# Index scores and attention logits taking two PSUM banks in turn, with four conditioning blocks moved in front of attention

## The chip, the cores and the metric

The kernel runs on one core of a Trainium2 chip. The metric is the device time of one execution in microseconds (us). The core's engines, as the profile names them, are TensorE (PE, matmuls and transposes), VectorE (DVE), ScalarE (ACT), GpSimd (POOL) and SyncE (SP, which only issues DMA transfers here). Each takes its instructions in a fixed order. Matmuls write to PSUM, which the kernel uses as eight banks of 128 x 512 floats.

## The reference, cut to what matters

Two blocks run one after the other on 256 tokens of width 1024. The change lies in the first one and in what feeds the second:

```
dots = relu(einsum('bqhd,bsd->bqhs', qi, ki));  score = einsum('bqhs,bqh->bqs', dots, wi) * idx_scale
sel  = top_k(score, 64)                              # visible keys only
logits = q.k * scale + rel_bias[bucket];  probs = softmax(logits over sel);  y_att = (probs @ v) @ w_att_out
y_conv = silu(layer_norm(depthwise_conv(a * sigmoid(g)) + conv_b)) @ w_conv_out
x = x + (sigmoid(gates0) * y_att + sigmoid(gates1) * y_conv) @ w_out
...                                                  # 128 gathered experts per token, a gated projection
sh1, sc1, g1, sh2, sc2, g2 = split(silu(c) @ ada_w + ada_b)   # "ada"; the same for c_ctx
...                                                  # second block: scan mixer and FFN, modulated by these
```

Here silu(c) @ ada_w is a vector of 1024 times a matrix of 1024 x 6144, for two vectors (c and c_ctx) in the first four of its twelve blocks ("rows" in the code) of 512 columns, and for c alone in the others.

## The kernel before

The program is written in code order, and a scheduler turns this order into a priority: it sets ahead of time the fixed sequence of each engine. Instructions from further down move up where an engine would otherwise wait. A tile whose buffer is still in use makes its writer wait, so buffer counts and PSUM banks shape these sequences.

PSUM is handed out by `bank(tag)`: four banks for large products ("mm"), two for transposes ("tp"), and one each under the tags "ac0" and "ac1". With the tag "ac" it takes "ac0" and "ac1" in turn:

```
in_turn = cycle(("ac0", "ac1"))
if tag == "ac":
    tag = next(in_turn)
```

The first block's code, in order, after the projections for the index:

- `index(t)` for the two halves of 128 tokens (t = 0, 1): four groups of two matmuls (L637) into bank "ac0"; ACT applies relu (L641, tile rl, two buffers), DVE sums heads (L646, L648) and finds the top 64 (L656, L657), giving the mask negm.
- the GLU products, then q, k and v (L211 with tiles wr and big; L600 are the transposes of q and k).
- `attention(t)`: SP loads the bias (L566, one buffer of tile bias, so the second half's load waits until PE has read the first half's); four groups of logits (L675 bias, L676 q.k) into "ac0"; DVE adds the mask into the tile lg (L678, one buffer); DVE takes the maximum (L682), ACT the exponentials (L685); for each head PE transposes (L691), ACT copies (L693) and PE multiplies by v (L695) into `po`, a bank "ac0" too; DVE normalizes (L698, tile ot); L249/L251 transpose it into aT.
- the gates: 64 matmuls of 512 columns (L211), taken by DVE (L753) and ACT (L754).
- the depthwise convolution yc on DVE (L759, L762), 120 multiply-adds.
- four blocks of `ada_row` for both vectors: SP loads wada in pieces of 512 KB (L398, two buffers, four for each block); ACT makes the first product (L405) and DVE 14 multiply-adds (L407) into two acc tiles (one buffer each); PE sums over partitions with eight one-column matmuls (L412, shown by the trace as 16) into bank "ac1".
- the convolution's layer norm (L767 to L784), two more blocks of ada for one vector, then att_out (L211 with aT), conv_out (L211 with yc) and the product with w_out. I call what begins with the aT products behind attention the last stretch.

The trace shows each float32 matmul as two records; "x8" in its rows is four matmuls.

Of the kernel before, what the change touches and what calls it, by code (L numbers as in the profile page):

```python
# [92 lines left out]
def block_kernel(ctx: ExitStack, tc: tile.TileContext, I, out):  # L93
# [21 lines left out]
    def bank(tag="mm", bufs=4, shape=(128, 512), name=None):  # L115
        if tag == "ac":
            tag = next(in_turn)
        if tag in ("ac0", "ac1"):
            bufs = 1
        return ps.tile(list(shape), F32, tag=tag, bufs=bufs, name=name or tag)  # L120
# [20 lines left out]
    def V(n):  # L141
        o, w = _V[n]
        return vec[:, o:o + w]
# [243 lines left out]
    def run(*gens):  # L387
        for _ in together(*gens):
            pass
# [156 lines left out]
    with ExitStack() as st:  # L546
# [82 lines left out]
        def index(t):  # L629

            S = 128 * (t + 1)
            score = p1.tile([128, 256], F32, tag="score", name="score", bufs=1)
            for g in range(2):
                for s in range(2):
                    p = bank("ac0")
                    for b in range(2):
                        nc.tensor.matmul(p[:, b * S:(b + 1) * S],  # L637
                                         qiT[s * 64:(s + 1) * 64, 2 * g + b, t * 128:(t + 1) * 128],
                                         kiT[s * 64:(s + 1) * 64, :S], start=True, stop=True)
                    rl = p1.tile([128, 512], F32, tag="rl", name="rl", bufs=2)  # L640
                    nc.scalar.activation(rl[:, :2 * S], p[:, :2 * S], AF.Relu)  # L641
                    for b in range(2):
                        h = 2 * (2 * g + b) + s
                        r = rl[:, b * S:(b + 1) * S]
                        if h == 0:
                            nc.vector.tensor_scalar(score[:, :S], r, wi[:, t, 0:1], None, op0=OP.mult)  # L646
                        else:
                            nc.vector.scalar_tensor_tensor(score[:, :S], r, wi[:, t, h:h + 1], score[:, :S],  # L648
                                                           op0=OP.mult, op1=OP.add)
            nc.vector.scalar_tensor_tensor(score[:, :S], score[:, :S], idx_scale, vis[:, t, :S],  # L650
                                           op0=OP.mult, op1=OP.add)
            work = p1.tile([128, 256], F32, tag="work", name="work", bufs=1)
            m8 = sm.tile([128, 8], F32, tag="m8", name="m8", bufs=2)
            cur = score
            for _ in range(8):
                nc.vector.max(out=m8, in_=cur[:, :S])  # L656
                nc.vector.match_replace(out=work[:, :S], in_to_replace=m8, in_values=cur[:, :S], imm_value=GONE)  # L657
                cur = work
            negm = p1.tile([128, 256], F32, tag="negm", name="negm", bufs=2)
            nc.vector.tensor_tensor(negm[:, :S], work[:, :S], score[:, :S], op=OP.is_equal)  # L660
            nc.vector.tensor_scalar(negm[:, :S], negm[:, :S], -1.0e30, None, op0=OP.mult)
            NM[t] = negm

        def attention(t):
# [3 lines left out]
            lg = p1.tile([128, H, S], F32, tag="lg", name="lg")  # L668
            for g in range(2):
                for s in range(2):  # L670
                    p = bank("ac0")
                    for b in range(2):
                        h = 2 * (2 * g + b) + s
                        o = p[:, b * S:(b + 1) * S]
                        nc.tensor.matmul(o, flip, bias[t][:, h], start=True, stop=False)  # L675
                        nc.tensor.matmul(o, qT[s * 64:(s + 1) * 64, 2 * g + b, t * 128:(t + 1) * 128],  # L676
                                         kT[s * 64:(s + 1) * 64, 2 * g + b, :S], start=False, stop=True)
                    nc.vector.tensor_tensor(lg[:, 4 * g + s:4 * g + s + 3:2, :],  # L678
                                            p[:, :2 * S].rearrange("p (s k) -> p s k", s=2),
                                            negm[:, None, :S].to_broadcast([128, 2, S]), op=OP.add)  # L680
# [3 lines left out]
            for h in range(H):  # L684
                nc.scalar.activation(lg[:, h], lg[:, h], AF.Exp, bias=nmx[:, h:h + 1], accum_out=se[:, h:h + 1])  # L685
            nc.vector.reciprocal(se, se)
            po = bank("ac0")
            for h in range(H):
                tr = tp_bank()
                for j in range(t + 1):  # L690
# [20 lines left out]
        nc.vector.tensor_scalar(qg8, V1("qg"), 0.125, None, op0=OP.mult)  # L711
        for t in range(NT):
            index(t)

        ohb = p1.tile([32, 512], F32, tag="sq", name="ohb", bufs=2)
        nc.sync.dma_start(out=ohb, in_=I["oh"])
# [8 lines left out]

        u = p1.tile([128, 4, TAPS - 1 + 256], F32, tag="u", name="u")
        nc.vector.memset(u[:, :, :TAPS - 1], 0.0)
        sc2 = scv.rearrange("p k s -> p (k s)")
        nc.scalar.activation(sc2, V("c"), AF.Sigmoid)
        nc.vector.tensor_tensor(sc2, sc2, V("c"), op=OP.mult)  # L730
        for j in range(4):
            p = bank()
            lin1(hT, I["w_glu"][2 * j], 256, p[:, :256])
# [6 lines left out]
        lin2(hT, 8, [W[4 * 2 + s] for s in range(4)], both,  # L740
             lambda t, p: nc.scalar.activation(vt[:, t], p, AF.Copy))

        pada = pool("pada", stack=st)
        for t in range(NT):
            attention(t)

# [11 lines left out]
        for j in range(4):  # L758
            nc.vector.tensor_scalar(yc[:, j], u[:, j, 0:256], cw[:, j, 0:1], V1("cb")[:, j:j + 1],  # L759
                                    op0=OP.mult, op1=OP.add)  # L760
            for k in range(1, TAPS):
                nc.vector.scalar_tensor_tensor(yc[:, j], u[:, j, k:k + 256], cw[:, j, k:k + 1], yc[:, j],  # L762
                                               op0=OP.mult, op1=OP.add)
        run(chain(*[ada_row(pada, j, 2) for j in range(4)]))
        pm = bank()
        for j in range(4):
            nc.tensor.matmul(pm[:, :256], mean, yc[:, j], start=j == 0, stop=j == 3)  # L767
# [15 lines left out]
        warm(AF.Sqrt, sgc[:, 0, 0:1])  # L783
        nc.vector.tensor_tensor(yc, yc, sgc, op=OP.mult)  # L784
        cT = yc,
        run(chain(*[ada_row(pada, j, 1) for j in range(4, 6)]))


        mix = sgt[:, :, :D]
# [1035 lines left out]
```

## Time and profile before

| | us |
|---|---|
| runs of the kernel before (median of 3; lowest to highest) | 1593.75; 1590.28 to 1598.25 |
| the profiled execution, its own time | 1593.02 |
| its span in the trace | 1591.3 |
| PE busy in the span | 1363.7 (86%) |
| DVE, POOL, ACT busy | 1139.2, 600.4, 516.4 |
| mean granted clock of PE | 0.899 of full speed |

The span is what the trace covers; 1.7 us of the execution's own time lie around it. A busy share is a mean over very different stages: the first 278 us hold the first block's attention and convolution, some 1070 us behind 300 are the gathered experts and the scan, and the last 200 us the FFN. The granted clock is the share of full speed that PE was given.

### The profile page before, as it was taken

The numbers are of one execution on the slowest core, as the hardware profiler recorded it, in microseconds if no ns is written. First come the engines' busy times: TensorE is split into PE (matmuls) and PEld (weight loads), VectorE is DVE, ScalarE is ACT, GpSimd is POOL, SyncE is SP. The second block draws the span as 40 slices with busy tenths as digits, with TensorE's granted clock in tenths as the row PEclk, the third lists the DMA queues.
The fourth block names the chain that finished last, engine by engine and source line by source line (L and its number), as shares of the span: only waits on it lengthen the run. The fifth ranks groups of instructions, "written<-read, shape, count | busy, mean of one in ns | idle before, by whom it ended". The sixth has DMA issues, their size and how long they took to land. (4 is left out here: it accounts for less than half of the span.)

```text
span 1591.3 us, 26450 instructions
## 1 busy us (share of the span) xinstructions
PE 1363.7 (86%) x10140; PEld 889.3 (56%) x10140; DVE 1139.2 (72%) x2495; ACT 516.4 (32%) x1290; POOL 600.4 (38%) x599
## 2 busy tenths in 40 slices
PE   7999979888878888887884979988679898599997
PEld 5744554666435554545432335645344577399997
DVE  3991573699969888989665687787842966456676
ACT  3122230332243333333233242233232223244543
POOL 0000001245555655565542564254500211356663
PEclk9999959999988888878897989879889889799999
DMA  9545463698898999896997999979987541446561
GB/s 352 187 146 167 137 213 111 254 351 329 322 388 304 392 370 368 329 351 266 416 416 308 398 402 357 362 276 380 408 315 274 178 142 57 170 132 188 181 189 53
DMA packets 90197, 435.12 MB, mean 273 GB/s; under 512 B 9996, under 2 KB 14620, under 8 KB 57304
## 3 DMA queue, kind: packets, MB, share of 16 engines
q0 software_dynamic: 36864, 268.45, 42.8%
q1 hardware_dynamic: 52488, 163.67, 30.0%
q8 instruction: 80, 1.31, 0.3%
q10 hardware_dynamic: 720, 1.31, 0.2%
q14 instruction: 45, 0.37, 0.1%
HBM read 428.39 MB, written 5.01 MB: 272 GB/s over the span
## 5 line engine op out<-in xcount | busy, mean ns | idle before, releaser
L875 POOL DMA_INDIRECT G<-in_experts,eidx x256 | 335.2, 1309 | 356.9 <-DVE x L909 229.3
L880 DVE SCALAR_TENSOR_TENSOR G<-G,h 128x1024 f32<-128x1024 f32 x256 | 322.7, 1272 | 18.4 <-DMA G<-in_experts,eidx 14.9
L905 PE MATMUL ac<-G,dg 128*128 128x512 f32 x504 | 280.3, 705 | 51.4 <-ACT dg L903 51.1
L905 PEld LDWEIGHTS ac<-G,dg 128*128 128x128 f32 x504 | 108.6, 226 | 189.1 <-issue 115.0
L909 DVE SCALAR_TENSOR_TENSOR x<-G,ga,x 128x1024 f32<-128x1024 f32 (+1 forms) x131 | 169.8, 1297 | 1.9
L889 ACT ACTIVATE gd<-dots,gate 128x1 f32<-128x1 f32 x256 | 74.0, 290 | 276.9 <-DVE G L880 271.8
L200 POOL TENSOR_TENSOR wl<-wr,wh 128x1024 fp32r<-128x1024 f32 x50 | 122.4, 2463 | 109.5 <-ACT wh L198 105.8
L211 PE MATMUL mm<-wr,big 128*128 128x512 f32 (+1 forms) x352 | 146.6, 570 | 0.0
L211 PEld LDWEIGHTS mm<-wr,big 128*128 128x128 f32 x352 | 64.2, 192 | 71.8 <-issue 69.7
L407 DVE SCALAR_TENSOR_TENSOR acc<-wada,scv,acc 128x512 f32<-128x512 f32 x112 | 82.9, 770 | 28.9 <-DMA wada<-in_ada 21.7
L211 PE MATMUL mm<-bigl,wh 128*128 128x256 f32 x352 | 99.5, 283 | 1.1 <-DVE bigl L345 1.1
L211 PE MATMUL mm<-bigh,wh 128*128 128x256 f32 x352 | 99.6, 284 | 0.4 <-DVE bigh L344 0.4
L211 PE MATMUL mm<-bigh,wl 128*128 128x256 f32 x352 | 99.1, 283 | 0.0
L799 POOL TENSOR_TENSOR sgt<-sgt 128x512 f32<-128x512 f32 x4 | 5.0, 1271 | 242.4 <-DVE sgt L798 242.4
L1638 DVE SCALAR_TENSOR_TENSOR facc<-mm,vec,facc 128x189 f32<-128x189 f32 (+2 forms) x176 | 75.4, 430 | 25.1 <-ACT facc L1631 20.8
L198 ACT ACTIVATE wh<-wr 128x1024 fp32r<-128x1024 f32 x66 | 69.6, 1059 | 71.8 <-PE tp L211 25.4
L211 PEld LDWEIGHTS mm<-bigl,wh 128*128 128x128 f32 x352 | 67.3, 191 | 1.9 <-DVE bigl L345 1.4
L211 PEld LDWEIGHTS mm<-bigh,wh 128*128 128x128 f32 x352 | 67.5, 192 | 1.4 <-DVE bigh L344 0.6
L211 PEld LDWEIGHTS mm<-bigh,wl 128*128 128x128 f32 x352 | 67.2, 191 | 0.4
L211 PE MATMUL mm<-wr,Xh 128*128 128x512 f32 x144 | 66.2, 609 | 0.0
L903 ACT ACTIVATE dg<-ident,ga 128x128 f32<-128x128 f32 x126 | 44.0, 393 | 28.6 <-DVE ga L892 23.3
L762 DVE SCALAR_TENSOR_TENSOR yc<-u,vec,yc 128x256 f32<-128x256 f32 x120 | 52.3, 475 | 0.3
(481 smaller groups left out, 2688.5 us busy)
## 6 DMA issues: line engine op xcount, KB each, us to landing
wr<-in_w_in SPq DMA_DIRECT2D x56, 512.0 KB
wada<-in_ada SPq DMA_DIRECT2D x48, 512.0 KB
wr<-in_ffn_up SPq DMA_DIRECT2D x44, 512.0 KB
wr<-in_ffn_down SPq DMA_DIRECT2D x22, 512.0 KB
wr<-in_w_att SPq DMA_DIRECT2D x16, 512.0 KB
wr<-in_w_gates SPq DMA_DIRECT2D x16, 512.0 KB
wr<-in_w_ple_gate SPq DMA_DIRECT2D x16, 512.0 KB
wr<-in_w_peer_q SPq DMA_DIRECT2D x14, 512.0 KB
```

The source lines that it names most:

```text
L198: nc.scalar.activation(wh[:, :n], w[:, :n], AF.Copy)
L200: e.tensor_tensor(wl[:, :n], w[:, :n], wh[:, :n].bitcast(F32), op=OP.subtract)
L211: nc.tensor.matmul(o, a, b, start=start and i == 0, stop=stop and i == len(l) - 1)
L407: nc.vector.scalar_tensor_tensor(acc[i], wv, c, acc[i], op0=OP.mult, op1=OP.add)
L762: nc.vector.scalar_tensor_tensor(yc[:, j], u[:, j, k:k + 256], cw[:, j, k:k + 1], yc[:, j], op0=OP.mult, op1=OP.add)
L875: ins = nc.gpsimd.indirect_dma_start(out=b, out_offset=None, in_=I["experts"], in_offset=bass.IndirectOffsetOnAxis(ap=eidx[t, h][:, n:n + ...
L880: nc.vector.scalar_tensor_tensor(b[:, :D], b[:, :D], 1.0, h2[t], op0=OP.mult, op1=OP.mult, accum_out=dots[:, n - g:n - g + 1])
L889: nc.scalar.activation(dg_[:, n:n + 1], dots[:, n:n + 1], AF.Copy, scale=gate[t, h][:, g + n:g + n + 1])
L903: nc.scalar.activation(dg, ident, AF.Copy, scale=c)
L905: nc.tensor.matmul(pacc[q], dg, v[:, q * 512:(q + 1) * 512], start=first and n == to_pe[0], stop=h == H - 1 and n == TOPK - 4)
L909: end = nc.vector.scalar_tensor_tensor(x[:, t, q], v[:, q], c, x[:, t, q], op0=OP.mult, op1=OP.add).ins
L1638: nc.vector.scalar_tensor_tensor(o, pg_[:, a0 + dy:a1 + dy, b0 + dx:b1 + dx], fw[:, j, k_:k_ + 1], o, op0=OP.mult, op1=OP.add)
```

## The change

Three tags become "ac": the index groups, the logit groups and `po` take both banks in turn. The silu of c, the pool of ada and ada's first four blocks stand right behind `index` in the code, with the tag "ac" too, instead of behind the convolution; the last two blocks keep their place and take "ac". The arithmetic is the same. Behind the change, code lines have numbers higher by 1 to 5 up to L763 and the same numbers from L767 on; rows of the kernel before go by its own lines.

```
 def index(t): ...
-                    p = bank("ac0")
+                    p = bank("ac")
...
 def attention(t): ...
-                    p = bank("ac0")
+                    p = bank("ac")
...
-            po = bank("ac0")
+            po = bank("ac")
...
         for t in range(NT):
             index(t)
+        sc2 = scv.rearrange("p k s -> p (k s)")
+        nc.scalar.activation(sc2, V("c"), AF.Sigmoid)
+        nc.vector.tensor_tensor(sc2, sc2, V("c"), op=OP.mult)
+        pada = pool("pada", stack=st)
+        run(chain(*[ada_row(pada, j, 2, tag="ac") for j in range(4)]))
...
-        sc2 = scv.rearrange("p k s -> p (k s)")
-        nc.scalar.activation(sc2, V("c"), AF.Sigmoid)
-        nc.vector.tensor_tensor(sc2, sc2, V("c"), op=OP.mult)
...
-        pada = pool("pada", stack=st)
...
-        run(chain(*[ada_row(pada, j, 2) for j in range(4)]))
...
-        run(chain(*[ada_row(pada, j, 1) for j in range(4, 6)]))
+        run(chain(*[ada_row(pada, j, 1, tag="ac") for j in range(4, 6)]))
```

The scheduler's sequences change well beyond these lines. On PE, at the end of the gates, the sequence of before has the first softmax's transposes (L691) and products with v (L695, bank ac_668) between gate matmuls (L211 mm<-wr,big), and the first ada block's sums (L412, ac_1101) behind them:

```order
L211 MATMUL mm<-wr,big 128x512 x12
L691 MATMUL tp<-ident,lg 128x128 x2
L211 MATMUL mm<-wr,big 128x512 x10
L695 MATMUL ac_668<-vt,pT 128x64 x2
L691 MATMUL tp<-ident,lg 128x128 x2
L211 MATMUL mm<-wr,big 128x512 x5
L412 MATMUL ac_1101<-cst,acc 128x1 x5
```

In the changed kernel the sums of ada's first four blocks (L412, ac_407 to ac_518) stand further up, among the products for q, k, v and the gates. At the end of the gates PE's sequence now reads as follows; ac_798 is the last logit group of the first half, ac_868 the first one of the second half, ac_816 the first half's product with v:

```order
L211 MATMUL mm<-wr,big 128x512 x5
L767 MATMUL mm<-yc,mean 128x256 x4
L675 MATMUL ac_798<-bias,flip 128x128
L676 MATMUL ac_798<-kT,qT 128x128
L675 MATMUL ac_798<-bias,flip 128x128
L676 MATMUL ac_798<-kT,qT 128x128
L773 MATMUL mm<-sqc,mean 128x256 x4
L691 MATMUL tp<-ident,lg 128x128 x2
L675 MATMUL ac_868<-bias,flip 128x256
L676 MATMUL ac_868<-kT,qT 128x256
L675 MATMUL ac_868<-bias,flip 128x256
L676 MATMUL ac_868<-kT,qT 128x256
```

So the last logits and the whole first softmax moved behind the gates, and the second half's first logits, which need the second bias, stand in front of the first half's products with v (L695, the next row).

On DVE, around the second half's maximum (L682 nmx), the sequence of before mixes the mask additions (L678) with ada's multiply-adds (L407):

```order
L407 SCALAR_TENSOR_TENSOR acc<-wada,scv,acc 128x512 x7
L678 TENSOR_TENSOR lg<-ac_738,negm 128x2x256
L407 SCALAR_TENSOR_TENSOR acc<-wada,scv,acc 128x512 x2
L682 TENSOR_REDUCE nmx<-lg 128x8
L407 SCALAR_TENSOR_TENSOR acc<-wada,scv,acc 128x512 x3
L686 RECIPROCAL se<-se 128x8
L364 TENSOR_TENSOR mcol<-ac_1175,vec 128x4 x2
L407 SCALAR_TENSOR_TENSOR acc<-wada,scv,acc 128x512 x14
L698 TENSOR_TENSOR ot<-ac_756,se 128x512
```

In the changed kernel the same place reads:

```order
L678 TENSOR_TENSOR lg<-ac_868,negm 128x2x256
L779 TENSOR_SCALAR yc<-yc,vec_172 128x256 x4
L698 TENSOR_TENSOR ot<-ac_816,se 128x512
L678 TENSOR_TENSOR lg<-ac_880,negm 128x2x256
L784 TENSOR_TENSOR yc<-yc,sgc 128x1024
L678 TENSOR_TENSOR lg<-ac_874,negm 128x2x256
L794 TENSOR_TENSOR sgt<-mm,sgt 128x512
L678 TENSOR_TENSOR lg<-ac_886,negm 128x2x256
L682 TENSOR_REDUCE nmx<-lg 128x8
```

No multiply-add of ada stands in front of that maximum any more; seven (of the sixth block) stand behind it. SP's sequence has ada's wada loads of the first four blocks among the loads for the gates, and the second bias behind seven wada, four att_out and three conv_out loads that follow the last gate loads. In the stages behind the first block the sequences of all engines differ in many places too, though no code there changed.

## Rows read from the trace of the kernel before

**Rows 1.** The page: its head.
```profile
span 1591.3 us, 26450 instructions
```

**Rows 2.** Windows by stage; columns: stretch, length, busy time of each engine, granted clock, DMA.
```profile
40.00:182.00 142.00, 142.00 (x458) 78.71 (x456) 86.31 (x233) 29.32 (x65) 0.00 (x0) 1.00 0.53 163
182.00:233.00 51.00, 39.05 (x158) 28.48 (x157) 41.03 (x66) 19.63 (x41) 0.00 (x0) 0.68 0.56 185
233.00:278.00 45.00, 44.66 (x126) 21.55 (x126) 16.08 (x26) 3.00 (x5) 4.99 (x4) 0.95 0.38 123
...
300.00:1367.00 1067.00, 876.70 (x7802) 539.24 (x7802) 826.37 (x1776) 345.35 (x977) 475.65 (x534) 0.87 0.85 328
```

**Rows 3.** Windows of 4 us around attention, same columns.
```profile
184.00:188.00 4.00, 3.47 (x17) 2.56 (x17) 4.00 (x8) 2.79 (x4) 0.00 (x0) 1.00 0.35 115
...
196.00:200.00 4.00, 4.00 (x24) 2.93 (x24) 2.73 (x7) 3.77 (x4) 0.00 (x0) 1.00 0.32 126
200.00:204.00 4.00, 2.00 (x5) 0.66 (x4) 3.28 (x6) 2.56 (x4) 0.00 (x0) 0.50 0.18 44
...
236.00:240.00 4.00, 4.00 (x8) 1.59 (x8) 2.96 (x4) 0.00 (x0) 0.00 (x0) 0.80 0.47 120
```

**Rows 4.** Timeline of PE, end of the gates: start, length, instructions, idle before.
```profile
151.46 0.38 PE L675 MATMUL ac<-bias,flip 128*128 128x128 f32 x2
...
172.23 0.55 PE L695 MATMUL ac<-vt,pT 128*128 128x64 f32 x4
...
172.85 4.46 PE L211 MATMUL mm<-wr,big 128*128 128x512 f32 x10
...
184.53 1.99 PE L773 MATMUL mm<-sqc,mean 128*128 128x256 f32 x8 [1.66 <-ACT sqc L770]
```

**Rows 5.** Timeline of PE, attention(1): same columns.
```profile
189.20 3.70 PE L211 MATMUL mm<-wr,aT 128*128 128x512 f32 x8
...
196.07 1.95 PE L412 MATMUL ac<-cst,acc 128*128 128x1 f32 x16
197.88 0.68 PE L675 MATMUL ac<-bias,flip 128*128 128x256 f32 x2
...
202.73 1.22 PE L675 MATMUL ac<-bias,flip 128*128 128x256 f32 x2 [2.00 <-DVE lg L678]
...
212.71 1.18 PE L691 MATMUL tp<-ident,lg 128*128 128x128 f32 x4 [5.31 <-ACT lg L685]
213.68 3.52 PE L412 MATMUL ac<-cst,acc 128*128 128x1 f32 x16
...
227.51 3.81 PE L412 MATMUL ac<-cst,acc 128*128 128x1 f32 x16 [1.42 <-DVE acc L407]
...
232.97 5.96 PE L211 MATMUL mm<-wr,aT 128*128 128x512 f32 x8 [0.69 <-ACT aT L251]
```

**Rows 6.** Timeline of DVE: maximum of attention(0).
```profile
153.59 1.22 DVE L682 TENSOR_REDUCE nmx<-lg 128x8 f32<-128x1024 f32 x1
```

**Rows 7.** Timeline of DVE, attention(1).
```profile
209.74 2.28 DVE L682 TENSOR_REDUCE nmx<-lg 128x8 f32<-128x2048 f32 x1
...
222.73 5.39 DVE L407 SCALAR_TENSOR_TENSOR acc<-wada,scv,acc 128x512 f32<-128x512 f32 x8 [1.10 <-DMA wada<-in_ada]
228.04 0.68 DVE L698 TENSOR_TENSOR ot<-ac,se 128x512 f32<-128x512 f32 x1
```

**Rows 8.** Timeline of ACT: exponentials of attention(0), a table load.
```profile
154.84 0.40 ACT L685 ACTIVATE lg<-lg,nmx 128x128 f32<-128x128 f32 x1 [4.82 <-DVE nmx L682]
...
184.49 1.28 ACT L775 ACT_TABLE_LOAD   x1
```

**Rows 9.** Timeline of SP's queue: DMA issues.
```profile
152.71 0.38 SPq L566 DMA_DIRECT2D bias<-brd  x1
...
181.62 24.06 SPq L398 DMA_DIRECT2D wada<-in_ada  x6
```

**Rows 10.** Window behind the issue of the second bias, columns as in Rows 2.
```profile
152.70:157.50 4.80, 4.80 (x13) 2.29 (x14) 1.65 (x2) 2.65 (x14) 0.00 (x0) 1.00 0.86 243
```
## Prediction

> **What bounds the kernel now.** I read the windows by stage first [rows 2]. From 40 to 182 us PE is busy all the time at full clock, so that stretch is as long as its matmuls. From 182 to 233 PE is busy for only 39.05 of 51.0 us and its granted clock is .68: this stretch, attention's second half, is paced by waits and by a slow clock. From 233 to 278 PE is again nearly always busy (44.66 of 45). Then comes the long stretch of gathered experts and scan, which the change does not touch in code.
>
> The 4 us windows [rows 3] show that the clock is binary here: 1.00 up to 200 us, .50 from 200 (1.2 GHz in place of 2.4 GHz) and 1.00 again only within the window from 236 on. The timeline of PE [rows 4, 5] shows what stands in between. The gates end with the row at 172.85 (4.46 us long), so at 177.2. PE waits 1.66 us for the conv's square, 2.00 us for DVE to empty the single logits bank, 5.31 us for the second softmax, 1.42 us for ada's DVE work and 0.69 us for aT. Between these waits stand three rows of one-column ada matmuls: 1.95 us at full clock, 3.52 and 3.81 at half. The last stretch starts at 232.97. I measure the change by how far this start moves.
>
> **The change, part by part.** All times below start from the profiled execution (1593.02 us, of which the span is 1591.3 [rows 1]). The median of the runs is 0.7 us higher, and I add that at the end.
>
> *Gates.* The sums of ada's first four blocks now stand in front of the end of the gates. One costs 197.88 - 196.07 = 1.8 us at full clock [rows 5], four cost 7.2. They delay the gates' end; in exchange the first half's last logit group (1.6 us, four rows from 151.46 on [rows 4]) and the transposes and products with v among the last gate matmuls (172.23 to 172.85, .6) leave. The gates end at 177.2 + 7.2 - 2.2 = 182.2. This holds if the acc tiles are ready in time. DVE was busy for 86.31 of 142 us in this stretch [rows 2]; the 42 multiply-adds of blocks 2 to 4 cost 42 x .67 = 28 us (5.39 us for eight [rows 7]), which makes 114 of 142. There is room on average. With such durations along the two sequences I estimate that the second block's acc is ready between 110 and 115 us and PE at its sums at 117: 2 us of margin at the tightest place. I take no wait, and at most 5 us.
>
> *From the gates to the second half's logits.* PE does the mean (1.8 us; the row of the same shape at 184.53 has 1.99 with its tail [rows 4]) to 184.0, and the last logits to 185.6. DVE adds the mask, to 186.2, and takes the maximum (1.22 us [rows 6]), to 187.4. The conv's subtraction and square take some 2.4 us (an estimate from the wait in front of 184.53), to 186.4; PE's second mean runs to 188.4. ACT loads its table (1.28 us) and makes eight exponentials in some .39 us each [rows 8], 187.7 to 190.9, then another table and a root, to some 192.6, and only then copies for the product with v.
>
> The second half's first logit group needs the second bias. SP issues that load when PE has read the first bias, at 185.6; in the kernel before the same load (8 x 256 floats on 128 partitions, 1.05 MB) was issued at 152.71 [rows 9], and the 4.8 us behind that moved 4.8 x 243 KB = 1.17 MB in all, with the DMA engines .86 busy [rows 10]. I take 4.6 us, bounded by 3.7 (the same at a share of 1) and 8.6 (half of that rate). So the group runs from 190.2 to 192.7. The products with v stand behind it in PE's sequence, but their copies come at 192.6 anyway: this wait hides behind ACT. They go at ACT's pace, I estimate .4 us for each head, to 196.0.
>
> *Second half's logits.* The next group (in the bank that the first logits leave) starts at 196.4, when DVE has written lg, which has one buffer and is free after the last transpose. A group is 2.5 us at full clock. The third needs ot and goes at 199.3, the aT products take 3.6 us (3.70 with the tail [rows 5]), to 205.4, and the fourth group ends at 207.9. In the kernel before the last group ended at 207.4, at half clock and after a 2.00 us wait for its bank: four rows of 1.22 against .68 us [rows 5]. So by 207.9 the 5.0 us lost in front of the gates' end have been won back.
>
> *Softmax and products of the second half.* Before, the maximum started at 209.74 and took 2.28 us [rows 7], because multiply-adds of ada stood in front of it. Now it can start as soon as the last mask addition is done, at 208.5, and ends at 210.8; the exponentials follow and PE's first transposes go at 211.4, against 212.71. Then PE ran one ada row of some 3.4 us among them, and one of 3.7 behind them after a 1.42 us wait [rows 5]. Both are gone. Without them the products take 226.1 - 212.7 - 3.4 = 10.0 us at half clock, to 221.4. Before, DVE was still in ada's multiply-adds (222.73 to 228.1) when they ended, so ot came at 228.04 [rows 7]; now it follows at 221.5. After ot, its transposes and ACT's copy (2.9 us, as from 221.5 to the start; before, from 228.04 with the 3.7 us ada row among them, 4.9) the last stretch starts at 224.3 in place of 232.97: **8.7 us earlier**.
>
> *Last stretch.* It held two one-column rows, of eight records each: half of the 1.95 us row, so .9 each [rows 5]. One leaves into the softmax wait, the other stands just in front of the first aT products, where PE waits for aT. I take 1.2 us of gain (0 to 1.8).
>
> *Bank alternation of the index scores.* PE never waited for their bank (it is busy 142 of 142 us [rows 2]), so this is worth 0: the GLU products fill the time between groups either way.
>
> The sum is -8.7 - 1.2 = -9.9 us: 1593.0 - 9.9 = 1583.1, and **1584 us** on the scale of the median.
>
> **The rivals.**
>
> *The clock falls early.* The sum takes full clock up to 207.9. In favour: the clock held at 1.00 through 184 to 188 with 3.47 of 4 us busy, just behind a wait of 1.66 us [rows 3, 4], and it fell at 200 in a stretch with a one-column row [rows 5], which now stands elsewhere. Against: the first softmax stood under gate matmuls and now stands behind them, so PE has some 2.6 us of waits between 185.6 and 190.2 and thin work from 192.5 to 196. If the clock falls at 190, four logit groups cost 2.1 us more each and the aT products 2.2 (5.96 - 3.70): 10.6 us if it stays down to the end, and the whole gain is gone, 1594. If it comes back within the dense groups, half: 1589. The Trainium skill, "TensorE: Matmul & The Clock Gate", section "A second HAM failure mode: psum-queue depth-cycling", says that a kernel that goes through PSUM banks in turn with small PE pauses between groups can make the clock swing between its levels. That speaks for this rival, and by it the time would be the 1589 to 1594 just worked out; the trace so far shows the fall in a stretch with one bank and pauses, so pauses, not banks, are what it lets me count.
>
> *The second bias comes late (slower).* In SP's sequence seven wada loads stand among the seven loads of att_out and conv_out in front of it, behind the last gate load. Before, six wada loads took 24.06 us from the first issue to the last one's end [rows 9], 4.8 us from one to the next, since each waits for DVE to free a buffer. If the first five are issued while PE still does the gates and two are late at that pace, the bias is issued at about 195 in place of 185.6, and everything behind it, the first half's products with v included, is 10 us late: no gain, 1594. Four late loads give 1603. It decides from an issue at 195 on. Against it: by the 114 of 142 us above DVE has 28 us to spare by 182, so the loads should be consumed as they land.
>
> *Ada's acc late in front of PE.* At about 117, 146 and 168 us by my estimate PE stands at ada's sums with the products of the gates behind them; a late acc costs its delay one to one. With 2 us of margin a 5 us error costs 3: 1587.
>
> *The gain is lost later.* From 300 to 1367 PE is busy 876.70 of 1067 us and the DMA engines .85 [rows 2]. The stretch starts earlier, but the sequences there differ in many places; a shift of some 5 us either way (half a per cent of it) would turn 1584 into 1589 or 1579. Nothing in the profile says which way, or that it could not be more: it runs at that DMA share, where another sequence of loads can also delay the gathers.
>
> **How the numbers follow.** About 8 us (0.5%) is what a measurement can tell from no change. Chances: the sum .45 (range of its own 1577 to 1589, from a shift of 5 us later and the bounds of the bias and the last stretch); the clock falls early .24 (1587 to 1595); the bias late .08 (1592 to 1604); acc late .07 (1584 to 1592); the gain lost later beyond 5 us .16 (1589 to 1608). Faster, below 1585.7, are three quarters of the first and some of the second and fourth: .40. Slower, above 1601.7, are half of the last, a third of the bias's case and a little of the clock's with a shift on top: .13. The rest, .47, lies within. The range 1576 to 1602 leaves out not quite 2 in 10, more of it above.
>
> **What would show it.** In the profile of the changed kernel: the gates' last matmul near 182; PE busy without a wait from 40 to 182; the second bias issued near 185.6; the granted clock 1.00 in the 4 us windows up to 208; the second maximum starting within 1 us of the last mask addition; no multiply-add of ada in front of the second ot; the last stretch starting near 224; and the 300 to 1367 stretch as long as before. A clock of .50 from 190 on, a bias issued behind 195, or idle PE in front of L412 between 110 and 170 would make the number wrong.

## The result, and the profile after

| | before | after |
|---|---|---|
| device time, median of 7 runs each (lowest to highest), us | 1592.96 (1590.28 to 1598.25) | 1603.38 (1597.73 to 1605.47) |
| ratio after to before, 95% interval | | 1.0058 [1.004, 1.0075] |
| the profiled execution's own time; its span | 1593.02; 1591.3 | 1597.73; 1596.0 |
| PE, DVE, POOL busy | 1363.7, 1139.2, 600.4 | 1355.1, 1142.6, 613.3 |
| mean granted clock | 0.899 | 0.896 |

The changed kernel is some 9 us longer by the ratio, 10.4 by the medians; 1584 with a range of 1576 to 1602 was forecast. The profiled execution of after is the shortest of its seven. Its trace therefore shows 4.7 us of the loss, and what the other six runs add (2 to 8 us) isn't in any trace.

The first view is the windows by stage of the kernel after, with the columns of [rows 2].

```profile
40.00:182.00 142.00, 141.07 (x483) 80.12 (x482) 115.56 (x284) 26.99 (x46) 0.00 (x0) 1.00 0.66 213
182.00:233.00 51.00, 42.81 (x144) 28.32 (x143) 18.33 (x27) 21.24 (x59) 0.00 (x0) 0.61 0.32 108
...
300.00:1367.00 1067.00, 869.35 (x7798) 540.24 (x7796) 824.96 (x1770) 344.14 (x971) 481.29 (x530) 0.87 0.84 325
```

From 40 to 182 PE is as good as always busy again. From 182 to 233 it is busy for 42.81 us in place of 39.05, at a clock of .61 in place of .68 and with 144 records in place of 158: it isn't more work, but slower work. The DMA share from 300 to 1367 is .84, against .85.

The 4 us windows of the kernel after show when the clock fell.

```profile
180.00:184.00 4.00, 2.69 (x12) 1.74 (x11) 1.65 (x3) 3.93 (x11) 0.00 (x0) 1.00 0.71 232
184.00:188.00 4.00, 2.64 (x7) 1.36 (x8) 0.78 (x2) 3.69 (x13) 0.00 (x0) 0.85 0.11 36
188.00:192.00 4.00, 4.00 (x17) 2.98 (x17) 2.40 (x2) 1.11 (x4) 0.00 (x0) 0.50 0.00 0
...
204.00:208.00 4.00, 4.00 (x6) 1.55 (x6) 0.43 (x1) 0.00 (x0) 0.00 (x0) 0.59 0.00 0
...
212.00:216.00 4.00, 1.44 (x10) 1.06 (x10) 3.97 (x6) 2.67 (x5) 0.00 (x0) 0.76 0.99 325
...
236.00:240.00 4.00, 4.00 (x8) 1.62 (x7) 0.69 (x1) 0.00 (x0) 0.00 (x0) 0.75 0.41 131
```

The clock falls at about 187, behind two windows in which PE had only 2.69 and 2.64 of 4 us of work. It stays at .50 through windows that are 4.00 of 4 us busy, and comes back at about 207. It falls once more at about 214, in the second softmax, and is down until about 238. Before, there was one fall, from 200 to about 238 [rows 3].

The timeline of PE in the kernel after answers to [rows 4, 5].

```profile
150.33 0.38 PE L675 MATMUL ac<-bias,flip 128*128 128x128 f32 x2
...
161.44 1.84 PE L412 MATMUL ac<-cst,acc 128*128 128x1 f32 x16
163.15 0.47 PE L675 MATMUL ac<-bias,flip 128*128 128x128 f32 x2
...
172.47 4.56 PE L211 MATMUL mm<-wr,big 128*128 128x512 f32 x10
...
185.36 0.67 PE L675 MATMUL ac<-bias,flip 128*128 128x256 f32 x2 [1.69 <-DMA bias<-brd]
...
187.60 1.22 PE L676 MATMUL ac<-kT,qT 64*128 64x256 f32 x2
...
210.73 0.70 PE L676 MATMUL ac<-kT,qT 64*128 64x256 f32 x2
...
215.99 1.18 PE L691 MATMUL tp<-ident,lg 128*128 128x128 f32 x4 [1.01 <-ACT lg L685]
219.70 1.12 PE L695 MATMUL ac<-vt,pT 128*128 128x64 f32 x4 [2.53 <-ACT pT L693]
...
232.02 6.63 PE L211 MATMUL mm<-wr,aT 128*128 128x512 f32 x8
```

Read the starts. The first half's logits begin at 150.33 and go on at 163.15, right behind sums of ada (L412, 161.44 + 1.84). The gates end at 172.47 + 4.56 = 177.0. The second half's first logit group starts at 185.36 after a wait of 1.69 us for the bias, and its last matmul of 64x256 has 1.22 us: the clock is down. The fourth group ends at 211.4, the transposes of the second softmax start at 215.99, the products with v wait another 2.53 us for ACT's copies, and the last stretch starts at 232.02. Before it was 232.97 [rows 5]: 0.95 us earlier, where 8.7 were forecast.

Where the two executions gain and lose is read from the starts of four instructions: PE's aT product (L211) that opens the last stretch, POOL's first and last gather of experts (L875), and PE's first matmul of L1544 with the tiles wr and m, in the FFN.

| us | last stretch | first gather | last gather | L1544 | span |
|---|---|---|---|---|---|
| before | 232.97 | 291.3 | 1142.5 | 1369.9 | 1591.3 |
| after | 232.02 | 290.0 | 1145.2 | 1376.9 | 1596.0 |
| after less before | -0.95 | -1.3 | +2.7 | +7.0 | +4.7 |

At its end the changed stretch is 1.3 us ahead. The gathers, from first to last, take 855.2 us against 851.2; from there to the FFN the scan takes 231.7 against 227.4; the FFN gives 2.3 back. No code in these stages changed. A place where single waits grew shows between 780 and 900 us, first in the kernel after, then in the kernel before (columns: engine, tile and line, what it waited for; us in total, times, longest):

```profile
POOL G L875 <- DVE x L909: 60.5, 11, 30.4
...
PE tp L324 <- DVE diag L311: 25.4, 1, 25.4
...
ACT ple_s L1347 <- DMA Ed<-ple_e: 19.3, 1, 19.3
```

```profile
POOL G L875 <- DVE x L909: 60.5, 12, 24.9
...
PE tp L324 <- DVE diag L311: 20.4, 1, 20.4
...
ACT ple_s L1347 <- DMA Ed<-ple_e: 13.1, 1, 13.1
```

The longest wait of the gathers grew, while their total stayed at 60.5 us. ACT waits here for a buffer. A projection for the second block, ple_e, is made in two parts for the second half of the tokens (L1329), and each part is written to DRAM (L1331); it is read back only at L1337, behind 1000 us. The tile of each part has the tag "s", for which the pool has one buffer, and ple_s (L1347) has the same tag. So the second part waits until the first write has landed (15.5 us), and ple_s until the second has (19.3). PE's transposes (L324) hang on that, and behind PE the next gather. The timelines of SP's queue and of ACT, in the kernel after:

```profile
818.43 0.33 SPq L1331 DMA_DIRECT2D Ed<-ple_e  x1
820.57 26.68 SPq L194 DMA_DIRECT2D wr<-in_w_in  x8
849.88 0.33 SPq L1331 DMA_DIRECT2D Ed<-ple_e  x1
```

```profile
846.14 0.60 ACT L1329 ACTIVATE ple_e<-mm 128x512 f32<-128x512 f32 x1 [15.54 <-DMA Ed<-ple_e]
...
879.23 0.69 ACT L1347 ACTIVATE ple_s<-mm,rstd 128x512 f32<-128x512 f32 x1 [19.35 <-DMA Ed<-ple_e]
```

The same in the kernel before:

```profile
826.12 0.33 SPq L1331 DMA_DIRECT2D Ed<-ple_e  x1
```

```profile
825.49 0.60 ACT L1329 ACTIVATE ple_e<-mm 128x512 f32<-128x512 f32 x1 [10.06 <-DMA Ed<-ple_e]
```

In the kernel after the data of the second write is there at 846.7; the write stands behind eight loads of w_in, goes at 849.88, and ACT is released at 879.2, some 29 us later. In the kernel before the data is there at 826.1, and the write goes at once, behind seven loads; ACT is released at 855.0, again some 29 us later. So SP's order holds the issue up by 3.1 us in after and not at all in before; most of the wait is the way from issue to landing.

### The profile page after: what moved, and what is told of

The parts are those of the page before. It is cut to its first block, busy times and chain, and to the rows that moved or that the text cites. A ratio compares the mean times of both kernels' runs of the same rounds, so it can differ in the third digit from the quotient of the medians.

```text
span 1596.0 us, 26437 instructions
## 1 busy us (share of the span) xinstructions
PE 1355.1 (85%) x10140; PEld 889.2 (56%) x10140; DVE 1142.6 (72%) x2495; ACT 515.6 (32%) x1289; POOL 613.3 (38%) x599
## 5 line engine op out<-in xcount | busy, mean ns | idle before, releaser
L875 POOL DMA_INDIRECT G<-in_experts,eidx x256 | 337.6, 1319 | 352.6 <-DVE x L909 216.6
L905 PE MATMUL ac<-G,dg 128*128 128x512 f32 x504 | 271.2, 682 | 51.1 <-ACT dg L903 50.8
L905 PEld LDWEIGHTS ac<-G,dg 128*128 128x128 f32 x504 | 103.7, 218 | 178.4 <-issue 105.6
L211 PE MATMUL mm<-wr,big 128*128 128x512 f32 (+1 forms) x352 | 144.5, 565 | 0.0
L211 PEld LDWEIGHTS mm<-wr,big 128*128 128x128 f32 x352 | 63.6, 190 | 70.7 <-issue 68.9
L211 PE MATMUL mm<-bigh,wh 128*128 128x256 f32 x352 | 99.3, 283 | 1.8 <-DVE bigh L344 1.8
L211 PE MATMUL mm<-bigl,wh 128*128 128x256 f32 x352 | 99.4, 283 | 0.2 <-DVE bigl L345 0.2
L211 PE MATMUL mm<-bigh,wl 128*128 128x256 f32 x352 | 99.3, 283 | 0.0
L407 DVE SCALAR_TENSOR_TENSOR acc<-wada,scv,acc 128x512 f32<-128x512 f32 x112 | 83.0, 758 | 21.9 <-DMA wada<-in_ada 18.6
L211 PEld LDWEIGHTS mm<-bigh,wh 128*128 128x128 f32 x352 | 67.3, 191 | 2.6 <-DVE bigh L344 2.0
L211 PEld LDWEIGHTS mm<-bigl,wh 128*128 128x128 f32 x352 | 67.4, 191 | 0.8 <-DVE bigl L345 0.4
L211 PEld LDWEIGHTS mm<-bigh,wl 128*128 128x128 f32 x352 | 67.3, 191 | 0.6
L211 PE MATMUL mm<-wr,Xh 128*128 128x512 f32 x144 | 67.0, 616 | 0.0
L763 DVE SCALAR_TENSOR_TENSOR yc<-u,vec,yc 128x256 f32<-128x256 f32 x120 | 53.1, 473 | 0.2
L324 PE MATMUL tp<-diag,x 128*128 128x128 f32 x96 | 17.0, 350 | 41.6 <-DVE diag L311 32.1
```

The costliest lines, as they stand in the source:

```text
L211: nc.tensor.matmul(o, a, b, start=start and i == 0, stop=stop and i == len(l) - 1)
L324: nc.tensor.matmul(p[:, j * 128:(j + 1) * 128], b, diag, start=True, stop=True)
L407: nc.vector.scalar_tensor_tensor(acc[i], wv, c, acc[i], op0=OP.mult, op1=OP.add)
L875: ins = nc.gpsimd.indirect_dma_start(out=b, out_offset=None, in_=I["experts"], in_offset=bass.IndirectOffsetOnAxis(ap=eidx[t, h][:, n:n + ...
L905: nc.tensor.matmul(pacc[q], dg, v[:, q * 512:(q + 1) * 512], start=first and n == to_pe[0], stop=h == H - 1 and n == TOPK - 4)
```

## The experiments

Two theories stood against each other. **The later sequence:** the change gains a little in front, and the scheduler's new sequences for the stages behind it, which nobody asked for, lose more. **The front:** the fallen clock, the late softmax and the shared banks eat the gain, and the rest is scatter. The kernels ran on three chips, each beside the kernel before on the same chip (medians of before: 1577.4 us for e1 to e4, 1578.4 for e5 to e8, 1594.9 for e9 to e12). Ratios are to that. The kernel after wasn't run beside any of them, and the kernel before alone differs by 1.1% between them; so a comparison of ratios from two chips is weaker than one from the same chip.

Where an experiment fixes the sequence of the later stages, it adds this helper behind the kernel's last instruction. From the first instruction of the experts on it chains each engine's instructions in a given order; it adds no waits on the chip. e9 fixes the whole program in this way. The helper, cut to what matters:

```
+        at = {i.name: i for i in nc.cur_bb.bb.instructions}
+        for names in SEQUENCE.values():
+            row = [at["I-%d" % n] for n in names]
+            for a, b in zip(row, row[1:]):
+                tc.add_manual_dep(b, a.name, NoSync, reason="keep_late")
```

**The two halves apart.** The first run (e1) is the changed kernel with the later sequence of before, the second (e2) the kernel before with the later sequence of after.

```
 # e1, on the kernel after
+SEQUENCE = LATER_OF_BEFORE
 # e2, on the kernel before
+SEQUENCE = LATER_OF_AFTER
```

> The changed kernel's first block, with each engine's sequence from the experts on forced to be that of the kernel before (edges that fix the issue order alone, no waits). Theory S, the new sequence of the later stages costs the time: the front's gain of about 1 us stays, ratio .998 to 1.001, experts start near 290 and the product L1544 m near 1369. Theory F, the new front itself makes the later stages slower (its state, its transfers): ratio 1.004 to 1.008 as for the changed kernel, L1544 m near 1377.

Measured: 0.9978 [0.9957, 0.9998].

> The kernel before up to the product with w_out, with each engine's sequence from the experts on forced to be that of the changed kernel. Theory S: ratio 1.005 to 1.009, the experts start at 291 as before and L1544 m comes near 1378. Theory F: ratio .998 to 1.002.

Measured: 1.0106 [1.0078, 1.0134]. The later sequence loses by itself, and the changed front by itself gains 0.2% (its interval ends just below 1). The spans of the two profiled executions differ by 18.2 us: 1.3 in front, 11.3 in the gathers (846.7 against 835.4 us), 8.0 from there to the FFN, and -2.4 in the FFN. The waits between 780 and 900 us, first with the sequence of before (e1), then with that of after (e2):

```profile
POOL G L875 <- DVE x L909: 56.1, 9, 25.3
...
PE tp L324 <- DVE diag L311: 21.9, 1, 21.9
...
ACT ple_s L1347 <- DMA Ed<-ple_e: 13.5, 1, 13.5
```

```profile
POOL G L875 <- DVE x L909: 56.1, 10, 30.3
...
PE tp L324 <- DVE diag L311: 25.4, 1, 25.4
...
ACT ple_s L1347 <- DMA Ed<-ple_e: 19.3, 1, 19.3
```

Both kernels show the waits that belong to the sequence, whichever front they have: 13.5 and 21.9 with the old one, 19.3 and 25.4 with the new one. The total of the gathers' waits in this window is the same 56.1 us in both, so how much of these waits reaches the end isn't shown by them.

**Parts of the change alone**, with the later sequence of before. In the first (e3), only the index groups, the logits and `po` take "ac", and ada stays where it was; in the second (e4), ada's four blocks move and keep a bank of their own, "ac1"; the third (e8) adds alternating index groups to that.

```
 # e3, in index(t) and attention(t)
-    p = bank("ac0")
+    p = bank("ac")
...
-    po = bank("ac0")
+    po = bank("ac")
 # e4 and e8, right behind index
+        run(chain(*[ada_row(pada, j, 2) for j in range(4)]))    # the default tag is "ac1"
 # e8 also, in index(t)
-    p = bank("ac0")
+    p = bank("ac")
```

> Only the banks in turn for index scores, logits and product with v; ada stays behind the convolution; the later stages' sequence forced to that of the kernel before. Theory: paired index groups in two banks run together and save 2.7 us of PE, the wait of 2.0 us for the single logits bank goes; ada's DVE work and one-column rows still stand in attention, so the last stretch starts 3 to 5 us earlier than 232.97, ratio .997 to .999. Rival, the clock falls earlier when the banks alternate: no gain, ratio .999 to 1.002, granted clock .50 before 200 us.

Measured: 1.0075 [1.0053, 1.0098], slower, which neither expectation had. The timeline of PE in e3:

```profile
215.12 5.88 PE L211 MATMUL mm<-wr,aT 128*128 128x512 f32 x8
...
301.63 1.83 PE L412 MATMUL ac<-cst,acc 128*128 128x1 f32 x8 [15.96 <-DVE acc L407]
```

The last stretch starts at 215.12, 17.9 us earlier than before, and the first gather at 284.2. What was won was ada's work, pushed back: PE now waits 15.96 us for an acc at 301.63, in front of the end of the first block, and the experts' first matmul (L905) goes some 14 us late. An early last stretch is no gain while the sums that were taken out of it are still owed.

> Only ada's first four blocks moved in front of the GLU products (bank ac1), index and attention on the one bank ac0; later stages' sequence as in the kernel before. Theory, taking ada out of attention helps if softmax stays under the gates: last stretch 4 to 9 us earlier, ratio .994 to .998. Rival, the first softmax moves behind the gates as in the changed kernel, and the clock falls near 187: ratio .999 to 1.002.

Measured: 0.9974 [0.996, 0.9989]. In e4 the first half's logits start at 134.88 and the last stretch at 229.83. The first softmax ends behind the gates here too, but the clock holds at 1.00 to about 212, though PE is busy for only 2.04 of 4 us from 192 to 196.

> As in e4 (ada moved in front, its sums in ac1, attention in ac0), and the index scores take both banks in turn; later sequence of the kernel before. Theory: paired index groups run at the same time on PE, 2.5 to 3 us off; the experts start 2 to 4 us earlier than in e4 (287.4), ratio .993 to .997. Rival: the pairs save nothing, since PE waits for something else by the last stretch: ratio as e4, .997.

Measured: 0.9966 [0.9949, 0.9982]; the first gather goes at 284.2 against 287.4 in e4. The 3.2 us are near what the pairs of index groups are worth below, but the two kernels ran on different chips, and the ratios do not tell them apart.

**SP's sequence, and the one write.** The first (e5) is the changed kernel with only SP's later sequence that of before; the second (e6) keeps all sequences of after but moves the second write of ple_e in front of the eight loads; the third (e11) does the same to the kernel before, and nothing else.

```
 # e5: SEQUENCE = LATER_OF_AFTER, and for SP alone LATER_OF_BEFORE
 # e6 (after), e11 (before): on SP
 L1331 DMA Ed<-ple_e
+L1331 DMA Ed<-ple_e
 L194 DMA wr<-in_w_in x8    (x7 in e11)
-L1331 DMA Ed<-ple_e
```

> The changed kernel as it is, but with SP's sequence of DMA issues from the experts on forced to be that of the kernel before; PE, DVE, ACT and POOL keep the changed kernel's sequences. Theory D, the later loss comes from how SP's loads stand around the two writes of ple_e to DRAM (L1331): the two waits of ACT for them (L1329 and L1347, 15.5 + 19.3 us in the changed kernel, 10 + 13 in the kernel before) fall to some 23 to 26 us together and the ratio to .998 to 1.002. Rival, the compute engines' sequences cost it: waits as in the changed kernel, ratio 1.004 to 1.009.

Measured: 1.0083 [1.0064, 1.0103]. This is what the rival expected: with SP's order of before the loss stays, so SP's order isn't what makes the later sequence slow, or not alone. ACT still waits 16.0 and 15.5 us for the two writes. That a mixture of two sequences costs something of its own isn't excluded.

> The changed kernel as it is, with one move in SP's sequence: the second write of ple_e (L1331) stands in front of the eight w_in loads, not behind them. Theory D: the wait for the second write (L1347, 19.3 us) shrinks by 4 to 11 us, ratio 1.000 to 1.003 against the changed kernel's 1.006. Rival: the write is late because of the gathers and of loads issued earlier, the waits stay, ratio 1.004 to 1.009.

Measured: 1.0006 [0.9991, 1.002]. SP's timeline, and the waits between 780 and 900 us in e6:

```profile
814.47 27.67 SPq L1331 DMA_DIRECT2D Ed<-ple_e  x2
842.23 7.09 SPq L194 DMA_DIRECT2D wr<-in_w_in  x8
```

```profile
POOL G L875 <- DVE x L909: 41.9, 12, 12.5
...
PE tp L324 <- DVE diag L311: 4.4, 1, 4.4
```

ACT's wait at L1347 is gone, PE's fell from 25.4 to 4.4, the longest gather wait from 30.4 to 12.5. The write, issued at about 842, has now landed when ACT comes to L1347 at 854.9, some 13 us later. The move changes two things at once: SP's queue keeps its order, so the eight loads also stand back until the write has its data (842.23 in place of 820.57). Which of the two helps wasn't separated, and a second buffer for the tag "s", which should take away both of ACT's waits, wasn't tried.

> The kernel before in all sequences, with that one move on SP alone: the second write of ple_e in front of the seven w_in loads. Theory D: the 13 us wait at L1347 goes, of which 5 to 10 us reach the end: ratio .993 to .997. Rival: the hole is filled by the next wait, .998 to 1.002.

Measured: 0.9921 [0.9892, 0.995]. So the move is worth at least as much to the kernel before (0.8%) as to the kernel after (0.5% between 1.0058 and 1.0006, on different chips). It is a loss that both have. In the traces of e1 and e2 the waits there differ by 3.5 us at PE (25.4 - 21.9) and 5.0 at the gathers (30.3 - 25.3), which is less than half of the 11.3 us by which the gathers differ.

**Ada's sums elsewhere.** One tag in the changed kernel:

```
-        run(chain(*[ada_row(pada, j, 2, tag="ac") for j in range(4)]))
+        run(chain(*[ada_row(pada, j, 2, tag="tp") for j in range(4)]))
```

with the later sequence of before (e7), with that sequence and the write in front (e10), and with nothing but this line, so that the scheduler makes its own later sequence (e12).

> The changed kernel's first block with one edit, the sums of ada's first four blocks go to the tp banks, so that attention's logits do not queue behind ada for ac0 and ac1; the later sequence is that of the kernel before. Theory B, in the changed kernel attention was held up by sharing its two banks with ada: the first logits start before 125 us (150 in the changed kernel), both softmaxes' first halves hide under the gates, the last stretch starts near 219 (232.0), the experts near 278, ratio .990 to .994. Rival: what held attention up was DVE's work, not the bank: logits start near 150, experts near 288, ratio .997 to 1.000.

Measured: 0.991 [0.9885, 0.9934]. The timeline of PE in e7:

```profile
113.35 0.61 PE L675 MATMUL ac<-bias,flip 128*128 128x128 f32 x4
...
171.84 0.38 PE L691 MATMUL tp<-ident,lg 128*128 128x128 f32 x2
...
181.20 1.89 PE L767 MATMUL mm<-yc,mean 128*128 128x256 f32 x8
...
220.37 5.55 PE L211 MATMUL mm<-wr,aT 128*128 128x512 f32 x8
```

The logits start at 113.35 in place of 150.33, and the first softmax stands under the gates again (171.84). The mean that follows the gates goes at 181.20, the clock holds at 1.00 to about 204, and the last stretch starts at 220.37: 11.65 us earlier than in after. The first gather goes at 277.3.

> e7 (changed first block, ada's sums in the tp banks, old later sequence) with the second write of ple_e in front of the w_in loads on SP, as in e6. Theory: the two gains add, as they lie in different stages; e7's .991 less 5 to 12 us: ratio .983 to .988, experts from 277, the wait at L1347 gone. Rival: the loads held back behind the write are late for the products with w_in, ratio .990 to .996.

Measured: 0.9823 [0.9791, 0.9855], 1566.00 against 1594.94 us.

> e7's first block (ada's sums in the tp banks) with whatever later sequence the scheduler makes of it. If a later sequence is worth some 17 us by chance, as between e1 and e2, this lies anywhere from .985 to 1.003, with its experts at 277 as in e7 and the difference to e7 behind them; if the old later sequence is nothing special, it is within .003 of e7's .991.

Measured: 0.981 [0.9778, 0.9841], 1564.47 against 1594.94 us: with this one tag the changed kernel beats the kernel before by 1.9%. The waits between 780 and 900 us in e12:

```profile
ACT L1347 <- DMA Ed<-ple_e: 5.2, 1, 5.2
```

The later sequence that the scheduler makes here has a short wait of ACT and none of PE at that place. Whether it is better than the sequence of before isn't shown: its ratio is 1% lower than that of e7, but e7 ran on another chip, and there its median (1560.80 us) and its span (1558.1 against 1562.2) are the shorter ones. On its own chip e12 can't be told from e10, which has the sequence of before with the write moved.

**The clock.** The changed kernel, all sequences kept, with eight extra matmuls whose result is not used. The fixed sequence puts four where PE waits for the second bias, and one behind each of four L695 of the first half.

```
+        fill = bank()
+        for j in range(8):
+            nc.tensor.matmul(fill, ident, vt[:, 0], start=True, stop=True)
```

> The changed kernel with all its sequences kept, and eight further matmuls of 512 columns (their result is not used) on PE where it waits in the first softmax: four in front of the second half's first logits, one each behind four products with v. Theory C, the clock fell near 187 because of these waits: it stays 1.00 to about 208, the four logit groups take 2.5 us each again, the last stretch starts 4 to 8 us earlier than 232.0 though PE does 3.5 us more. Rival, the fall has another cause (banks in turn, or the waits before): the clock still falls before 195, the last stretch starts 1 to 4 us later.

Measured: 1.0048 [1.0028, 1.0068], which can't be told from after's 1.0058 [1.004, 1.0075]. The windows and the timeline of PE in e9:

```profile
184.00:188.00 4.00, 4.00 (x11) 1.88 (x11) 0.20 (x1) 3.97 (x15) 0.00 (x0) 1.00 0.23 74
188.00:192.00 4.00, 4.00 (x18) 2.36 (x18) 2.98 (x2) 0.81 (x5) 0.00 (x0) 1.00 0.00 0
...
204.00:208.00 4.00, 3.82 (x12) 1.65 (x10) 0.83 (x2) 0.00 (x0) 0.00 (x0) 1.00 0.00 0
```

```profile
184.16 3.60 PE L776 MATMUL mm<-vt,ident 128*128 128x512 f32 x8
187.60 0.59 PE L675 MATMUL ac<-bias,flip 128*128 128x256 f32 x2
...
207.13 0.70 PE L676 MATMUL ac<-kT,qT 64*128 64x256 f32 x2
...
228.40 5.61 PE L211 MATMUL mm<-wr,aT 128*128 128x512 f32 x8
```

The clock is 1.00 where it was .50, the fourth logit group ends at 207.8 in place of 211.4, and the last stretch starts at 228.40, 3.6 us earlier than in after, although the group with the second bias starts 2.2 us later, behind the extra matmuls. The front thus shows what the clock was worth. The total doesn't follow: the first gather goes 4.6 us earlier than in after, but the span is 3.0 us longer (1599.0), with 1.3 us more in the gathers, 1.5 in the scan and 4.8 in the FFN. Why was not followed up.

## Why the prediction was wrong, point by point

**The step that failed for the total** is the likeliest case's assumption that the stretch from 300 to 1367 would be "as long as before". The text had the rival, "the gain is lost later", and wrote that "nothing in the profile says which way". It was given .16, and it decided the sign. With the two fronts exchanged, it is the later sequence that carries the loss (1.0106 on the old front, against 0.9978 for the new front on the old sequence). Where in that sequence most of it lies stays open. One place was found, the waits for the two writes of ple_e, longer by 3.5 us at PE and 5.0 at the gathers; but with SP's order of before the loss stays (e5), and moving the second write helps the kernel before as well (e11). The rest of the 11.3 us in the gathers and the 8.0 us behind them have no place. That the profile said nothing was a little too strong: the waits for Ed stood in the trace of before, and SP's two sequences show the write behind one load more. What that costs they don't say.

**In front** -9.9 us were forecast and -1.3 came at the first gather. The last stretch started at 232.0 in place of the forecast 224.3. The 7.7 us between them add up as follows; the first row is a gain that wasn't forecast and hides a part of the others.

| step of the sum | forecast | measured | off by |
|---|---|---|---|
| gates end | 182.2 | 177.0 | -5.2 |
| from there to the end of the fourth logit group | 25.7 | 34.4 | +8.7 |
| from there to the second softmax's transposes | 3.5 | 4.6 | +1.1 |
| transposes to the end of the products with v | 10.0 | 12.7 | +2.7 |
| from there to the last stretch | 2.9 | 3.3 | +0.4 |

- *Gates.* "Bank alternation … worth 0" was wrong. The timeline of PE for the index scores in the kernel after (the x8 are two groups in two banks), then in the kernel before:

```profile
47.23 0.72 PE L637 MATMUL ac<-kiT,qiT 64*128 64x128 f32 x8
...
52.39 1.14 PE L637 MATMUL ac<-kiT,qiT 64*128 64x256 f32 x8
```

```profile
48.34 0.71 PE L637 MATMUL ac<-kiT,qiT 64*128 64x128 f32 x4
...
65.09 1.13 PE L637 MATMUL ac<-kiT,qiT 64*128 64x256 f32 x4
```

Before, each group of four records took 0.71 us (64x128) or 1.13 us (64x256) by itself. Now eight records take 0.72 or 1.14. Three such pairs save 0.71 + 1.13 + 1.13, about 3 us; PE was busy all the time there, so that is its gain in full. Of the other 2.2 us, 1.5 are luck: this execution is ahead by that much before the first index group, mostly since its first products (L211, twelve records from 12.86) take 5.32 us against 6.63. That isn't the change, as they take 5.32 us in e11 too, whose first block is that of before. The last 0.7 us are not placed. The 7.2 us for ada's sums were right: one block takes 1.84 us.

- *To the fourth logit group.* The bias was right: issued at 179.84, 2.8 us behind the gates' end where 3.4 were forecast, the group 8.4 us behind it where 8.0 were. The step that failed is "full clock up to 207.9", with the 8.7 us of the table; the rival "the clock falls early" (.24) is what happened, with its waits at the place it named. The clock was down from about 187 to 207. Filled waits keep it up (e9). The Trainium skill, "TensorE: Matmul & The Clock Gate", section "A second HAM failure mode: psum-queue depth-cycling", speaks of small PE pauses while a kernel (there with bf16 products of 512 columns) goes through PSUM banks in turn. The runs agree with the pauses in it and not with the banks: e9 goes through the same banks in the same sequence and holds 1.00 to 208. (e7 takes the same two banks in turn for attention too and holds 1.00 to 204, but differs in more than the pauses.) Nor does each pause bring a fall: e4, with attention in one bank, held 1.00 through its window of 2.04 us. What the clock looks at was not measured.

- *Why the softmax was late at all.* The prediction took the first softmax behind the gates from the sequence, as given. The cause is that ada's sums and the logits share two banks in turn, so that logits queue behind sums whose acc is not made yet: 150.33, against 114.70 before and 113.35 with the sums in other banks (e7). That move is worth 11.65 us in front. Sharing isn't all of it: in e4 ada's sums and the logits have a bank each, and the logits start at 134.88.

- *Second softmax.* The maximum indeed starts at once (212.19) and ends at 214.48. The exponentials follow only at 215.34, since ACT loads its table (1.28 us) from 214.04 on, behind a product of ada; before, the table was loaded at 201.31. The forecast had no load there, which is most of the 1.1 us in the table. Then "without them the products take 226.1 − 212.7 − 3.4" took ada's row of 3.52 us as time on the path. It had stood in the shadow of ACT's eight exponentials; without it PE waits 2.53 us for pT. The first product follows the transposes after 3.71 us, against 4.35 before (212.71 to 217.06). Removing the row there gave 0.6 us, not 3.4.

- *To the last stretch.* One block of the sums, L412 with 1.71 us, now stands in front of the aT products. The last stretch itself (start to first gather) is 58.0 us against 58.3, where 1.2 less was forecast; why was not followed up.

**What held:** PE waits for less than 1 us between 40 and 182 (141.07 of 142 busy), so "ada's acc late" did not come (DVE is busy for 115.56 us there, where 114 was estimated), nor did "the second bias comes late" (its wait is the 1.69 us above).

## What to carry to other kernels

An instruction that stands between two others is a saving only if nothing else fills its time: look at which engine the next one waits for, and take the row out in thought before subtracting it. Sums that end a long chain should not share a rotation of banks with work that is ready early, since the order of the rotation makes the ready work wait. And where a scheduler rebuilds the whole program, its sequences for untouched stages can move by as much as the change is worth (e1 and e2 differ by 1.3%, on one chip), so compare the waits there, or hold that part fixed, before crediting or blaming the edit. Last, a wait that the profile puts down to a DMA write can be a wait for the buffer that the write reads: look at which tiles share its tag.

## What the runs showed of the hardware

- Two groups of matmuls with 64-row operands, in the two halves of the 128 rows and with two banks to write to, ran at the same time: eight records in 0.72 us, as against four in 0.71.
- In the kernel after, PE had no wait from 185.36 to 211.4, and yet the clock was at .50 (1.2 GHz) from about 187 to 207, through windows that were 4.00 of 4 us busy.
- The second write of ple_e in after, 256 KB issued at 849.88 behind eight loads of 512 KB, released ACT some 29 us later, with the DMA engines busy without a break (share 1.02 from 850 to 880). In e6, in front of the loads and at the same share, it took at most some 13 us. The bias, four times as large, was there 5.5 us behind its issue at 179.84.
